# One-pass shift products in the last normalisation, and nine unread matrix products behind the output projection

## The chip, the cores and the metric

The kernel runs on one core of a Trainium2 chip. The metric is the device time in microseconds (us) of one execution, as the median over several runs. Profiles are of one execution each, and their times count from its first instruction.

## The reference

The program is one layer of an encoder with 512 tokens and 2048 features: an input projection, two kinds of attention with gates, an output projection, and at the end a residual and a layer normalisation. Only the end matters here:

```python
out = jnp.einsum('bse,ed->bsd', y, w_out[layer])
x = _layer_norm(DEEPNORM_ALPHA * x + out, ln_gain[layer], ln_bias[layer])

def _layer_norm(x, g, b):
    mu = xf.mean(-1, keepdims=True)
    var = jnp.square(xf - mu).mean(-1, keepdims=True)
    return (xf - mu) * lax.rsqrt(var + LN_EPS) * g + b
```

With the reciprocal deviation rs and z = ALPHA x + out, a row of the output is z·g·rs + (−mu·rs)·g + b. The second and third terms, a column per token times the gain row plus the bias row, are called the shift below. It has rank two.

## The kernel before

**Stages.** The core works through input projections (a Strassen scheme), attention with the gates and part of the output projection as filler, and then the output projection alone. There the tokens lie in four tiles of 128 (`t` 0 to 3) and the features in four groups of 512 (`dc` 0 to 3). Half of the contraction has been summed earlier into `z[t][dc]`; the rest runs over units `u` 4 to 7. The groups `dc` 0 and 1 are done for all tiles first. Then all weights of `dc` 2 and 3 are held in SBUF as `wts` (tiles `wlast`), and the loop goes tile by tile: 24 matmuls of 512 columns for `dc` 2, 24 for `dc` 3, then the tile's normalisation on VectorE while TensorE goes on with the next tile. The very last group, `t` 3 and `dc` 3, is done in two halves of 256 columns in two PSUM banks (48 matmuls).

**Number kinds.** A matmul operand of fp32 precision is split into a high and a low part of kind fp32r by `split` (ScalarE copies the high part, VectorE subtracts), and three fp32r matmuls stand for one of fp32. Only a few small products are plain fp32; among them are the transpose and the three shift products of the last tile.

**The last tile.** Nothing is left for TensorE to do beside tile 3's normalisation, so `last_norm` (L889) gives part of it to TensorE. Groups 0, 1 and 2 of the tile have been multiplied by the gain before the mean is known. Once `bn_aggr` (L894), the root on ScalarE (L895) and the reciprocal (L911) are there, VectorE writes −mu·rs into column 0 of `nms` (L912); column 1 holds ones since the start of the kernel. TensorE transposes `nms` (L914), ScalarE copies the result to `left` (L917), and three products of two rows each (L920) make the shift of groups 2, 0 and 1 from `rows`. Those rows are the gain and bias as they lie in memory, fetched by six DMAs of 2 KB in `shift_rows` (L886). VectorE meanwhile does group 3 without them (`centre`, L899, then `rescale`, L905), and then `rescale` of groups 2 and 0 and of group 1 in two halves, each reading its shift from PSUM. Each `rescale` issues one store of its result, on the queues of SyncE and ScalarE in turn (L908).

**Order.** In the loop over the last tiles VectorE's order is the written one (`manual_schedule` for that engine); the orders of TensorE, ScalarE, GpSimd and of SyncE's DMA queue are laid down at build time by the framework's scheduler from a simulated timeline. `shift_rows` stands in the program after the fetches of x and before the eight fetches of `wts` (L954), outside the manual part.

**Space.** `slot("h0")` to `slot("h5")` are the buffers in which split weights rotate up to group 1; the shift rows and `left` reuse `h1`, `h2` and `h3`, so they wait for the last matmuls that read those. `u0` held temporaries of the attention. PSUM has banks `acc` (4), `sc` (2, pool `pss`) and `pt` (2, pool `pst`).

Of the kernel before, what the change touches and what calls it, by code (L numbers as in the profile page):

```python
# [6 lines left out]
F32 = mybir.dt.float32  # L7
F32R = mybir.dt.float32r
BF16 = mybir.dt.bfloat16
AF = mybir.ActivationFunctionType  # L10
ALU = mybir.AluOpType
# [48 lines left out]
def _view(t, offset, dims):  # L60
    return bass.AP(tensor=t.tensor, offset=t.offset + offset, ap=dims)
# [2 lines left out]
BLOCKS = (("k", 0), ("q", 0), ("v", 0), ("k", 1), ("q", 1), ("v", 1))  # L64
ORDER = [(m % 2, m // 2) for m in range(2 * PAIRS)]
EARLY = 6
BIAS = ((0, 24), (192, 32), (448, 24))
BW = 640


def hybrid_layer(tc, xT, xn, w_in, w_early, w_gate, w_out, t5x, brow, rpb, cmask, eye, gain, lbias, out):
    nc = tc.nc
    from contextlib import ExitStack
    with ExitStack() as ctx:
        const = ctx.enter_context(tc.tile_pool(name="const", bufs=1))
        arena = ctx.enter_context(tc.tile_pool(name="arena", bufs=1))
        small = ctx.enter_context(tc.tile_pool(name="small", bufs=4))
        dram = ctx.enter_context(tc.tile_pool(name="dram", bufs=1, space=bass.MemoryType.DRAM))
        pacc = ctx.enter_context(tc.tile_pool(name="pacc", bufs=4, space=bass.MemoryType.PSUM))
        pss = ctx.enter_context(tc.tile_pool(name="pss", bufs=2, space=bass.MemoryType.PSUM))  # L80
        pst = ctx.enter_context(tc.tile_pool(name="pst", bufs=2, space=bass.MemoryType.PSUM))

        def f(ap):
            return ap.bitcast(F32)

        def split(raw, hi, lo):
            nc.scalar.activation(hi, raw, AF.Copy)
            nc.vector.tensor_tensor(lo, raw, f(hi), ALU.subtract)
# [5 lines left out]
        def slot(tag, dtype=F32, name=None):  # L94
            return arena.tile([128, sizes[tag[0]]], dtype, name=name or tag, tag=tag)
# [10 lines left out]
        def bank(pool, name):  # L106
            tag = {id(pacc): "acc", id(pss): "sc", id(pst): "pt"}[id(pool)]
            return pool.tile([128, 512], F32, name=name, tag=tag)
# [13 lines left out]
        idle = bank(pss, "sc")  # L122
# [3 lines left out]
        ident = const.tile([128, 128], F32, name="ident")  # L126
# [37 lines left out]
        def prep_b(g):  # L164
# [13 lines left out]
            def table(v):  # L178
                r, masks = held
                w, o = BIAS[v][1], 16 if v == 0 else 8  # L180
                gt = slot("b1", F32, "gt")[:, :15 * w].rearrange("p (d j) -> p d j", d=15)
# [4 lines left out]
            def write(v):  # L186
                at, w = BIAS[v]
                for k in range(8):
# [14 lines left out]
        for tag, n, ops in (("s0", 4, A5), ("s1", 4, A5), ("c0", 2, A6), ("c1", 2, A6),  # L203
                            *((f"n{i}", 1, A6) for i in range(4)), *((f"n{i}", 1, A3) for i in range(4, 12))):
            t = slot(tag, F32R, "op").rearrange("p (n s q) -> p n s q", n=n, s=2)
# [61 lines left out]
        def plain_block(src):  # L267
# [3 lines left out]
            accs = [bank(p, "acc") for p in (pacc, pacc, pacc, pacc, pss, pss)]  # L271
            width = 128 * EARLY

# [9 lines left out]
            for i in range(8):  # L283
                xr = slot(f"r{i}", F32, "xraw")[:, :1024].rearrange("p (s q) -> p s q", s=2)
                raws.append(xr)
                for s in range(2):
                    k, n = i + 8 * s, 2 * i + s
                    if n == 0:
# [16 lines left out]
                        split(raw[:, far], w[0][:, far], w[1][:, far])  # L305
                        for jj in (range(2), range(2, EARLY)):
                            for c in (slice(0, HALF), slice(HALF, S)) if jj[0] == 0 else (slice(0, S),):
# [6 lines left out]
                    if n < 14:  # L314
                        for j in range(EARLY):
                            mms(n, k, w, j)
# [169 lines left out]
        sg_out, sg_ring, rc_ring, y_ring = Ring("n6"), Ring("n8", "n9"), Ring("n10", "n11"), Ring("n5", "n7")  # L486
        stream = [w_gate[i] for i in range(2 * (2 * PAIRS - EARLY))] + [w_out[8 * dc + u] for dc in range(4) for u in range(4)]
        raw_ring, raws, ready = Ring("r8", "r9", "c0", "c1"), [], []
# [125 lines left out]
        def scores(n):  # L614
# [14 lines left out]
            if g == 0:  # L629
                p, exponent = softmax(sc, biases[h][:, 48 - 16 * b:560 - 16 * b], 512, 0, i, 4 * a + b)  # L630
                probs[n] = p, 4
                return exponent
            at = BIAS[(0, 1, 1, 2)[b]][0]
            outer = {0: (64, outers[h % 2][0]), 3: (0, outers[h % 2][1])}
# [70 lines left out]
        yk, z = [], []  # L705
# [5 lines left out]
        def out_mms(acc, t, u, wh, wl, first, last, part=slice(0, 512)):  # L711
            c = slice(t * 128, t * 128 + 128)
            for kk in range(2):
                k = 2 * u + kk
                wk = slice(kk * 512 + part.start, kk * 512 + part.stop)
                for n, (s, w) in enumerate(((0, wh), (1, wh), (0, wl))):
                    nc.tensor.matmul(acc[:, part], yk[k][:, s, c], w[:, wk], start=first and kk == 0 and n == 0,  # L717
                                     stop=last and kk == 1 and n == 2)
                    yield
# [20 lines left out]
        def fillers():  # L740
            for j in range(EARLY, 2 * PAIRS):
                yield from gate_unit(j)
            z.extend([] for _ in range(4))
            for dc in range(4):
                yield from out_first(dc)
# [21 lines left out]
        with tc.manual_schedule(engines=engines):  # L767
# [6 lines left out]
            for n in range(136):  # L774
                b, i = n % 4, n // 8
# [14 lines left out]
                if mixing:  # L790
                    if exponent:
                        exponent()
                    mine, theirs, y, t = values(n // 4 - 1)
# [28 lines left out]
        for tiles, src, first in ((gb, gain, 0), (bb, lbias, 6)):  # L822
            for i in range(4):
                t = slot(f"n{first + i}", F32, "gain")
# [54 lines left out]

        def shift_rows():  # L880

            groups = slot("h1", F32, "lnrows"), slot("h2", F32, "lnrows")
            groups = groups[0][:, :512], groups[0][:, 512:], groups[1][:, :512]
            for r, src in enumerate((gain, lbias)):
                for c in range(3):
                    nc.sync.dma_start(groups[c][r:r + 1], src[:, 512 * c:512 * c + 512])  # L886
            return groups

        def last_norm(rows):  # L889

            t = 3
            mv = small.tile([128, 2], F32, name="mv", tag="mv")
            rs = small.tile([128, 1], F32, name="rs", tag="rs")
            nc.vector.bn_aggr(mv, st[t])  # L894
            nc.scalar.activation(rs, mv[:, 1:2], AF.Sqrt, bias=eps)  # L895

            def centre(i):
                zt = z[t][i]
                nc.vector.scalar_tensor_tensor(zt, zt, mv[:, 0:1], gb[i], op0=ALU.subtract, op1=ALU.mult)  # L899

            queues = [nc.sync, nc.scalar]

            def rescale(i, part, by):
                zt = z[t][i][:, part]
                nc.vector.scalar_tensor_tensor(zt, zt, rs, by, op0=ALU.mult, op1=ALU.add)  # L905
                queue = queues.pop(0)
                queues.append(queue)
                queue.dma_start(out[384:512, 512 * i + part.start:512 * i + part.stop], zt)  # L908

            whole = slice(0, 512)  # L910
            nc.vector.reciprocal(rs, rs)  # L911
            nc.vector.scalar_tensor_tensor(nms[:, 0:1], mv[:, 0:1], -1.0, rs, op0=ALU.mult, op1=ALU.mult)  # L912
            flat = bank(pst, "pt")[0:2, 0:128]
            nc.tensor.transpose(flat, nms, ident)  # L914
            shifts = []
            left = slot("h3", F32, "lnleft")[0:2, 0:128]
            nc.scalar.activation(left, flat, AF.Copy)  # L917
            for i in (2, 0, 1):
                c = bank(pacc, "acc")
                nc.tensor.matmul(c, left, rows[i][0:2], start=True, stop=True)  # L920
                shifts.append(c)
            centre(3)
            rescale(3, whole, bb[3])
            rescale(2, whole, shifts[0])
            rescale(0, whole, shifts[1])
            for part in (slice(0, 256), slice(256, 512)):
                rescale(1, part, shifts[2][:, part])
# [17 lines left out]
        load_x(1)  # L945

        rows = shift_rows()
        nms = small.tile([128, 2], F32, name="nms", bufs=1)
        nc.gpsimd.memset(nms, 1.0)
        wts = {}  # L950
        for dc in (2, 3):
            for u in range(4, 8):
                raw = out_ring.next("wraw")
                nc.sync.dma_start(raw[:, :1024], w_out[8 * dc + u])  # L954
                i = 2 * (u - 4)
                wts[dc, u] = [slot(f"{'tr'[dc - 2]}{i + m}", F32R, "wlast") for m in range(2)]
                split(raw[:, :1024], *wts[dc, u])
        for t in range(4):
            for dc in (2, 3):
                acc = bank(pacc, "acc") if dc == 2 else bank((pss, pst)[t % 2], "acc")  # L960
                parts = (slice(0, 256), slice(256, 512)) if (t, dc) == (3, 3) else (slice(0, 512),)
                accs = [acc] if len(parts) == 1 else [acc, bank(pss, "sc")]
                for o, part in zip(accs, parts):
                    for u in range(4, 8):
                        list(out_mms(o, t, u, *wts[dc, u], u == 4, u == 7, part))
                with tc.manual_schedule(engines={mybir.EngineType.DVE}):
                    if (t, dc) == (0, 2):
                        for i in range(2):
                            nc.vector.tensor_tensor(z[3][i], z[3][i], gb[i], ALU.mult)
                    residual(dc, t)  # L970
                    for m, part in enumerate(parts):
                        finish(dc, t, accs[m], part, dc + m)
                    if (t, dc) == (3, 2):
                        nc.vector.tensor_tensor(z[t][2], z[t][2], gb[2], ALU.mult)
                    if dc == 3 and t < 3:
                        norm(t)
                    elif dc == 3:
                        last_norm(rows)


def _weights(w_in, w_out):
# [11 lines left out]
    gate = [4096 * g + 3072 + 128 * j for g, j in ORDER]  # L993
    early = np.concatenate([w[order][:, :, c:c + 128] for c in gate[:EARLY]], axis=2)
    blocks = []
# [42 lines left out]
```

## Time and profile before

| | |
|---|---|
| median of 3 runs | 978.78 us (977.58 to 978.81) |
| the profiled execution's own time | 979.85 us |
| its span, first to last instruction | 978.1 us |
| granted TensorE clock, mean | 0.996 |
| TensorE busy | 968.9 us, 99% |
| VectorE busy | 753.8 us, 77% |
| ScalarE busy | 484.5 us, 50% |

The span is 1.75 us shorter than the execution's own time, because that also holds what lies around the first and last instruction. PE is TensorE, PEld its weight loads, DVE VectorE, ACT ScalarE, POOL GpSimd, SPq and ACTq the sequencers of SyncE and ScalarE as they issue DMAs. A busy share says little about a stage: for each stage one reads which wait ends last.

### The profile page before, as it was taken

To read this page: it belongs to the slowest core of one execution; us is meant where nothing else is said; L and a number is where in the kernel's file an instruction comes from. 1 tells how busy PE (TensorE), PEld (TensorE's weight loads), DVE (VectorE), ACT (ScalarE), POOL (GpSimd) and SP (SyncE) were. 2 spreads that over 40 slices of the span, in tenths; PEclk is the share of its full clock that TensorE was granted. 3 is DMA by queue.
4 is the path that set the end of the run, shared out by engine and by line. 5 is a ranking of instruction groups with operands and counts; after the bars stand their busy time and mean duration, and the time that the engine had idled before them with its cause. 6 is when DMAs were issued, how large, how long until landed. Compare 5 with 4: busy or idle time off the path is not lost.

```text
span 978.1 us, 13605 instructions
## 1 busy us (share of the span) xinstructions
PE 968.9 (99%) x4639; PEld 799.2 (82%) x4639; DVE 753.8 (77%) x1150; ACT 484.5 (50%) x837; POOL 180.2 (18%) x325
## 2 busy tenths in 40 slices
PE   9999999999999999999999999999999999999996
PEld 7887888888888888888888888888888888888885
DVE  7948788787988968978889567676776867778876
ACT  7544344334445434434454366666766666764200
POOL 1000665663553600000000001010011001000020
PEclk9999999999999999999999999999999999999998
DMA  9831788679769628527634967777768688769222
GB/s 345 297 108 60 173 253 264 205 232 253 204 191 301 183 86 270 144 93 214 157 125 125 348 180 213 207 228 228 193 206 247 186 235 217 192 224 312 66 78 95
DMA packets 116034, 194.13 MB, mean 198 GB/s; under 512 B 46373, under 2 KB 65573, under 8 KB 115964
## 3 DMA queue, kind: packets, MB, share of 16 engines
q1 hardware_dynamic: 103132, 169.13, 56.6%
q0 software_dynamic: 12256, 23.47, 8.8%
q8 instruction: 37, 0.61, 0.3%
q10 hardware_dynamic: 576, 0.66, 0.2%
q14 instruction: 33, 0.27, 0.1%
HBM read 148.69 MB, written 44.50 MB: 198 GB/s over the span
## 4 chain that ended last, share of the span: by engine, by line
PE 97%; ACT 1%; DVE 1%; issue 0%; POOL 0%; DVEq 0%; ACTq 0%; POOLq 0%
PE acc L389 16%; PE acc L391 16%; PE acc L390 16%; PE acc L717 14%; PE acc L523 11%; PE pv L669 4%; PE pt L647 4%; PE acc L278 2%; PE acc L279 2%; PE acc L280 2%; PE sc L628 2%; PE sc L627 2%; PE pt L259 1%; PE sc L717 1%; PE pt L717 1%; PE acc L920 0%
## 5 line engine op out<-in xcount | busy, mean ns | idle before, releaser
L372 ACT ACTIVATE wh<-braw 128x1024 fp32r<-128x1024 f32 x168 | 178.4, 1062 | 254.7 <-PE acc L390 203.6
L377 DVE TENSOR_TENSOR wl<-braw,wh 128x1024 fp32r<-128x1024 f32 x168 | 206.2, 1230 | 53.7 <-ACT wh L372 52.1
L389 PE MATMUL acc<-wh,xk 128*128 128x512 f32 x384 | 151.9, 396 | 0.0
L391 PE MATMUL acc<-wl,xk 128*128 128x512 f32 x384 | 149.8, 390 | 0.0
L390 PE MATMUL acc<-wh,xk 128*128 128x512 f32 x384 | 149.6, 390 | 0.0
L368 DVE TENSOR_TENSOR braw<-braw 128x1024 f32<-128x1024 f32 x96 | 116.8, 1217 | 0.0
L389 PE MATMUL acc<-wh,op 128*128 128x512 f32 x288 | 112.8, 392 | 0.0
L391 PE MATMUL acc<-wl,op 128*128 128x512 f32 x288 | 112.2, 390 | 0.0
L390 PE MATMUL acc<-wh,op 128*128 128x512 f32 x288 | 112.1, 389 | 0.0
L717 PE MATMUL acc<-wh,yk 128*128 128x512 f32 x320 | 108.2, 402 | 0.0
L653 DVE TENSOR_TENSOR tl<-pt,th 128x256 fp32r<-128x256 f32 (+1 forms) x128 | 71.0, 555 | 48.1 <-ACT th L652 46.7
L652 ACT ACTIVATE th<-pt 128x256 fp32r<-128x256 f32 (+1 forms) x128 | 62.4, 490 | 64.9 <-PE pt L647 62.8
L523 PE MATMUL acc<-xk,wh 128*128 128x512 f32 x320 | 90.8, 402 | 0.0
L391 PEld LDWEIGHTS acc<-wl,xk 128*128 128x128 f32 x384 | 72.1, 188 | 15.4
L389 PEld LDWEIGHTS acc<-wh,xk 128*128 128x128 f32 x384 | 72.1, 188 | 15.1 <-ACT bias L150 0.9
L390 PEld LDWEIGHTS acc<-wh,xk 128*128 128x128 f32 x384 | 72.2, 188 | 14.3
L584 DVE CUSTOM_DVE_ANT_0 s<-sc,biases 128x512 f32<-128x512 f32 (+2 forms) x128 | 68.0, 531 | 17.9 <-PE sc L628 17.3
L588 ACT ACTIVATE p<-s,mn 128x512 f32<-128x512 f32 (+1 forms) x96 | 62.1, 647 | 25.5 <-DVE mn L584 25.2
L717 PEld LDWEIGHTS acc<-wh,yk 128*128 128x128 f32 x320 | 58.4, 189 | 8.9
L523 PEld LDWEIGHTS acc<-xk,wh 128*128 128x128 f32 x320 | 57.0, 189 | 9.5
L160 POOL DMA_DIRECT2D bias<-rows_d x128 | 61.5, 487 | 17.3 <-DMA bias<-rows_d 5.5
L717 PE MATMUL acc<-wl,yk 128*128 128x512 f32 x160 | 64.0, 403 | 0.0
(164 smaller groups left out, 1656.1 us busy)
## 6 DMA issues: line engine op xcount, KB each, us to landing
braw<-in_w_in SPq DMA_DIRECT2D x96, 512.0 KB
wraw<-in_w_out SPq DMA_DIRECT2D x32, 512.0 KB
wraw<-in_w_gate SPq DMA_DIRECT2D x20, 512.0 KB
k_d<-kst SPq DMA_DIRECT2D x64, 128.0 KB
q_d<-kst SPq DMA_DIRECT2D x64, 128.0 KB
v_d<-vst SPq DMA_DIRECT2D x32, 256.0 KB
q<-q_d SPq DMA_DIRECT2D x32, 256.0 KB
k<-k_d SPq DMA_DIRECT2D x16, 512.0 KB
```

What stands on the lines that cost most here:

```text
L368: nc.vector.tensor_tensor(raws[q][u], raws[q][u], raws[other][u], ALU.add)
L372: nc.scalar.activation(h, raws[q][u], AF.Copy)
L377: nc.vector.tensor_tensor(l, raws[q][u], f(h), ALU.subtract)
L389: nc.tensor.matmul(accs[t], ah[:, q], h[:, c], start=k == 0, stop=False)
L390: nc.tensor.matmul(accs[t], al[:, q], h[:, c], start=False, stop=False)
L391: nc.tensor.matmul(accs[t], ah[:, q], l[:, c], start=False, stop=k == 7)
L523: nc.tensor.matmul(acc, w[:, k * 128:k * 128 + 128], X[8 * u + k][:, s], start=u == 0 and n == 0 and k == 0, stop=u == 1 and n == 2 and k ...
L584: nc.vector.tensor_tensor_reduce(*flat, bias, 1.0, 3e38, ALU.add, ALU.min, mn)
L588: nc.scalar.activation(p[:, to:to + n].rearrange("p (b r c) -> p b r c", r=8, c=c), s[:, :n].rearrange(order, r=8, c=c), AF.Exp, bias=mn, ...
L652: nc.scalar.activation(th, pt[:, :nch], AF.Copy)
L653: nc.vector.tensor_tensor(tl, pt[:, :nch], f(th), ALU.subtract)
L717: nc.tensor.matmul(acc[:, part], yk[k][:, s, c], w[:, wk], start=first and kk == 0 and n == 0, stop=last and kk == 1 and n == 2)
```

## The change

`shift_rows` fetches gain and bias in another layout: column 4c to 4c+3 of `raw` (gain) and 12 further (bias) hold four features of group c on each of the 128 partitions. `raw` is split into high and low parts of kind fp32r, and fifteen DMAs from SBUF to SBUF lay these out again as five rows for each of the three groups: gain high, gain low, gain high, bias high, bias low. In `last_norm` −mu·rs is written to a small tile `nm`, rounded to fp32r into columns 0 and 1 of `nms`, and the remainder goes into column 2; the other columns hold ones. The transpose yields eight rows instead of two, and the three products are fp32r with five rows. Behind the last matmul of the output projection stand nine more fp32r matmuls of 512 columns, into a bank `sc` that nothing reads.

```diff
+AWAKE = 9
 ...
         def shift_rows():
-            groups = slot("h1", F32, "lnrows"), slot("h2", F32, "lnrows")
+            raw, parts = slot("u0", F32, "lnraw"), slot("h0", F32R, "lnparts")
+            for i, src in enumerate((gain, lbias)):
+                nc.sync.dma_start(raw[:, 12 * i:12 * i + 12].rearrange("p (c j) -> p c j", c=3),
+                                  _view(src, 0, [[4, 128], [512, 3], [1, 4]]))
+            split(raw[:, :24], parts[:, :24], parts[:, 24:48])
+            groups = slot("h1", F32R, "lnrows"), slot("h2", F32R, "lnrows")
             groups = groups[0][:, :512], groups[0][:, 512:], groups[1][:, :512]
-            for r, src in enumerate((gain, lbias)):
+            for r, at in enumerate((0, 24, 0, 12, 36)):
                 for c in range(3):
-                    nc.sync.dma_start(groups[c][r:r + 1], src[:, 512 * c:512 * c + 512])
+                    nc.sync.dma_start(f(groups[c][r:r + 1]), f(parts[:, at + 4 * c:at + 4 * c + 4]))
             return groups
 ...
+            nm = small.tile([128, 1], F32, name="nm", tag="nm")
 ...
-            nc.vector.scalar_tensor_tensor(nms[:, 0:1], mv[:, 0:1], -1.0, rs, op0=ALU.mult, op1=ALU.mult)
-            flat = bank(pst, "pt")[0:2, 0:128]
-            nc.tensor.transpose(flat, nms, ident)
+            nc.vector.scalar_tensor_tensor(nm, mv[:, 0:1], -1.0, rs, op0=ALU.mult, op1=ALU.mult)
+            nc.vector.tensor_copy(nms[:, 0:2], nm.to_broadcast([128, 2]))
+            nc.vector.tensor_tensor(nms[:, 2:3], nm, f(nms[:, 0:1]), ALU.subtract)
+            flat = bank(pst, "pt")[0:8, 0:128]
+            nc.tensor.transpose(flat, f(nms), ident)
 ...
-            left = slot("h3", F32, "lnleft")[0:2, 0:128]
+            left = slot("h3", F32R, "lnleft")[0:8, 0:128]
 ...
-                nc.tensor.matmul(c, left, rows[i][0:2], start=True, stop=True)
+                nc.tensor.matmul(c, left[0:5], rows[i][0:5], start=True, stop=True)
 ...
-        nms = small.tile([128, 2], F32, name="nms", bufs=1)
-        nc.gpsimd.memset(nms, 1.0)
+        nms = small.tile([128, 8], F32R, name="nms", bufs=1)
+        nc.gpsimd.memset(f(nms), 1.0)
 ...
+                if (t, dc) == (3, 3):
+                    idle = bank(pss, "sc")
+                    for _ in range(AWAKE):
+                        nc.tensor.matmul(idle, yk[8][:, 0, 0:128], wts[3, 4][0][:, 0:512], start=True, stop=True)
```

## The prediction

> **What bounds the kernel now.** First the page's chain that ended last, then the chain piece by piece from 940 us on, then engines and granted clock by stage.
>
> ```profile
> PE 97%; ACT 1%; DVE 1%; issue 0%; POOL 0%; DVEq 0%; ACTq 0%; POOLq 0%
> ...
> 922.07 23.12 PE acc L717 x102
> ...
> 963.02 2.89 PE sc L717 x24
> 965.91 0.02 issue
> ...
> 966.85 0.30 DVE mv L894
> ...
> 967.18 0.30 ACT rs L895
> ...
> 967.51 0.17 DVE rs L911
> 967.68 0.02 issue
> 967.70 0.17 DVE nms L912
> 967.87 0.04 issue
> 967.92 0.28 PE pt L914
> ...
> 968.23 0.28 ACT lnleft L917
> ...
> 968.54 4.21 PE acc L920 x6
> ```
>
> Columns are start, length and what. Until 965.91 PE alone sets the time: 102 matmuls in 23.12 us, one each 0.227 us, no gap. What the change can win lies in the 12.2 us behind. There the chain is one of short steps, and one long piece, the shift products, 4.21 us. How much of that VectorE feels is in its own rows (start, duration, what, idle time before).
>
> ```profile
> 967.78 0.74 DVE L899 SCALAR_TENSOR_TENSOR z<-z,mv,gain 128x512 f32<-128x512 f32 x1
> 968.56 0.75 DVE L905 SCALAR_TENSOR_TENSOR z<-z,rs,gain 128x512 f32<-128x512 f32 x1
> 969.70 0.75 DVE L905 SCALAR_TENSOR_TENSOR z<-z,rs,acc 128x512 f32<-128x512 f32 x1 [0.39 <-PE acc L920]
> 971.07 0.75 DVE L905 SCALAR_TENSOR_TENSOR z<-z,rs,acc 128x512 f32<-128x512 f32 x1 [0.62 <-PE acc L920]
> 972.78 0.87 DVE L905 SCALAR_TENSOR_TENSOR z<-z,rs,acc 128x256 f32<-128x256 f32 x2 [0.96 <-PE acc L920]
> 973.18 0.47 DVE L905 SCALAR_TENSOR_TENSOR z<-z,rs,acc 128x256 f32<-128x256 f32 x1
> ```
>
> VectorE waits three times for a product, 0.39 + 0.62 + 0.96 = 1.97 us, and ends at 973.65. That is all that faster products can bring it, not 4.21 us. Behind it come the stores; here are their issues and, by quarter microseconds, the load of PE, PEld, DVE, ACT and POOL, then granted clock, DMA share and GB/s.
>
> ```profile
> 969.34 4.67 SPq L908 DMA_DIRECT2D out<-z  x3
> 970.49 3.15 ACTq L908 DMA_DIRECT2D out<-z  x2
> 973.68 0.33 SPq L908 DMA_DIRECT2D out<-z  x1
> ...
> 969.50:969.75 0.25, 0.25 (x2) 0.18 (x1) 0.05 (x1) 0.00 (x0) 0.00 (x0) 1.00 0.00 0
> 969.75:970.00 0.25, 0.25 (x2) 0.02 (x1) 0.25 (x1) 0.00 (x0) 0.00 (x0) 0.77 0.00 0
> 970.00:970.25 0.25, 0.25 (x2) 0.25 (x1) 0.25 (x1) 0.00 (x0) 0.00 (x0) 0.50 0.23 90
> 970.25:970.50 0.25, 0.25 (x1) 0.06 (x1) 0.20 (x1) 0.00 (x0) 0.00 (x0) 0.50 1.04 393
> 970.75:971.00 0.25, 0.25 (x2) 0.17 (x1) 0.00 (x0) 0.00 (x0) 0.00 (x0) 0.50 0.48 172
> 971.00:971.25 0.25, 0.25 (x2) 0.17 (x1) 0.18 (x1) 0.00 (x0) 0.00 (x0) 0.50 0.00 0
> 974.75:975.00 0.25, 0.00 (x0) 0.00 (x0) 0.00 (x0) 0.00 (x0) 0.00 (x0) 0.50 0.71 242
> 975.00:975.25 0.25, 0.00 (x0) 0.00 (x0) 0.00 (x0) 0.00 (x0) 0.00 (x0) 0.50 0.00 0
> ```
>
> A store's data flow some 0.87 us behind its issue (969.34, to about 970.2) at up to 393 GB/s, so 256 KB take 0.67 us, and between two stores the DMA engines now stand still. The last data flow until about 974.93, 1.28 us behind VectorE's end; the remaining 3.2 us to 978.1 are landing and closing, which the change leaves alone. The clock is full until 969.75 and half from 970.0.
>
> **The change, part by part.**
>
> *Two more small steps ahead of the transpose.* The row of `nm` takes the place of L912; a copy of two columns and a subtraction of one follow, each needing the one before. From L911 to L912, likewise dependent, it is 967.70 − 967.51 = 0.19 us from start to start. Neither step is in the trace; the bounds are 0.08 each, the gap from L912 to the independent L899 behind it, and 0.33, from L894 to L895 across engines. They stay on one engine and depend on each other, so I take 0.19 each. `nms` is ready at 967.87 + 0.38 = 968.25, and `centre` of group 3 starts at 967.78 + 0.38 = 968.16. This is a loss of 0.38 us on VectorE's path, hidden by nothing.
>
> *Transpose and copy.* Eight rows instead of two change neither the 128 streamed columns nor the copied ones: 0.28 and 0.28 as before, with the same gaps, so the first product starts at 968.54 + 0.38 = 968.92.
>
> *The products.* Six records stand for three products, two each; an fp32r product is one record.
>
> ```profile
> L717 PE MATMUL acc<-wlast,yk 128*128 128x512 f32 x168 | 38.2, 389 | 0.0
> L920 PE MATMUL acc<-lnrows,lnleft 2*128 2x512 f32 x6 | 4.2, 854 | 0.4 <-ACT lnleft L917 0.4
> 969.08 0.18 PEld L920 LDWEIGHTS acc<-lnrows,lnleft 2*128 2x128 f32 x1 [0.24 <-issue]
> ```
>
> With five rows it isn't in the trace. Its bounds are 0.39 us, the mean of 128 rows, and 1.16 us, the wait from 968.54 to VectorE's start at 969.70. I take 0.18 for the weights plus 0.39, as the rows say of the same kind with more rows: the shifts are ready at 969.49, then 0.227 us apart, 969.72 and 969.94.
>
> *VectorE then.* Dependent operations start 0.78 apart (967.78 to 968.56); for independent ones the row is one from the normalisation of the tile before.
>
> ```profile
> 960.79 0.74 DVE L856 SCALAR_TENSOR_TENSOR z<-z,rs,gain 128x512 f32<-128x512 f32 x1
> 961.45 0.74 DVE L852 SCALAR_TENSOR_TENSOR z<-z,mv,gain 128x512 f32<-128x512 f32 x1
> ```
>
> 0.66 to 0.67. So `centre` 968.16, `rescale` of group 3 968.94, group 2 969.61, group 0 970.28, group 1 970.95 and 971.35, end 971.82. Each shift is there 0.12, 0.56 and 1.01 us before it is read: the waits of 1.97 us go. Of the three product waits 0.38 us is given back by the small steps, and some 0.24 us is recovered by operations that now overlap at their ends: 973.65 − 971.82 = 1.83 us earlier.
>
> *The stores are late next.* They are issued at 969.72, 970.40, 971.06, 971.46 and 971.85. Data of the first flow from 970.59; at 0.67 us for each of three, and 0.33 for each half, the engines run without a pause until 970.59 + 2.67 = 973.26, which the last store alone, 971.85 + 0.87 + 0.33 = 973.05, would not need. So 0.2 us of the gain stays in the queue: 974.93 − 973.26 = **1.67 us**. Halves have rows of 1 KB; in the trace both took 0.75 us (974.18 to 974.93) rather than 0.67, which makes the gain 1.6. I take 1.6.
>
> *Nine unread matmuls.* At 0.227 us they take 2.04, from 965.91 to 967.95. `nms` comes at 968.25, so they lie in PE's wait, with 0.3 us to spare. Their bank was last read by tile 2, whose data VectorE took at 954.75. Cost nothing; if that cover fails, at most 2.04 us, if they stood ahead of the last matmuls. Their worth is near nothing too. Without them the clock would halve at about 969.88 again, when the three products have all started (968.92, 969.15, 969.37).
>
> Trainium skill, "TensorE: Matmul & The Clock Gate", part 1: after at least one idle window of about 3.4 us the clock falls to half, and the windows run free, so the moment can differ between runs. The trace shows the fall 3.97 us behind PE's last full work and does not show where the window began. By that rule the fall could come as early as 965.91 + 3.4 = 969.3 without the nine, and with them not before the products end; by the row nothing is won, and by the page at most one late product, 0.2 us, that VectorE reads only 1.01 us later. The sum is 1.6 us by both.
>
> *Fetching and splitting the rows.* Two fetches and fifteen copies between SBUF rows replace six fetches on SP's queue; one small ACT copy and one small DVE subtraction are new (0.27 and 0.16 by the nearest rows, L917 and L912), long before 968 and off PE's path. On SP stands behind them the last weight fetch, L954.
>
> ```profile
> 911.22 0.55 SPq L886 DMA_DIRECT2D lnrows<-in_gain  x2
> 914.89 0.35 SPq L954 DMA_DIRECT2D wraw<-in_w_out  x1
> 916.43 0.23 SPq L886 DMA_DIRECT2D lnrows<-in_gain  x1
> 919.08 1.23 DVE L88 TENSOR_TENSOR wlast<-wraw,wlast 128x1024 fp32r<-128x1024 f32 x1 [2.36 <-ACT wlast L87]
> 932.99 0.69 DVE L842 TENSOR_TENSOR z<-acc,z 128x512 f32<-128x512 f32 x1 [4.02 <-PE acc L717]
> L243 SPq DMA_DIRECT2D k_d<-kst x64: 574/605/1021, 130.2 to 407.1; - x64
> ```
>
> The weight is ready at 920.31 and first read by the last six matmuls of tile 0's group 3, at 932.97 − 6·0.227 = 931.6: 11.3 us of slack. The split can start when `h0` is free, as `h1` is, at 911.2, so copies start near 911.9. Issues of DMAs with several dimensions take 0.605 us here (extremes 0.574 and 1.021; a single row 0.23). Fifteen take 9.1 us: all of them ahead of L954 move it from 914.89 to 921, 6.1 late, and 5.2 us of slack are left. They cost nothing.
>
> *Sum.* 1.6 us. Against the profiled execution: span 976.5, own time 979.85 − 1.6 = 978.25. The median shown, 978.78, lies 1.07 us under that execution's own time; carried over, 978.78 − 1.6 = **977.2 us**. A measurement of this kernel tells about 0.2%, 1.96 us, from no change: 976.8 and 980.7.
>
> **The rivals.**
>
> *More than the sum (faster).* If the two small steps overlap like L912 and L899, at 0.08 us each, VectorE ends at 971.60; and if the stores' last data end 1.28 us behind it as now, the gain is 2.05 us: **976.7**. For it: every small operation in these rows overlaps where it may. Against: the steps depend on each other, and the stores have no pause left to save.
>
> *The products keep their length.* If five-row fp32r products took what fp32 takes at full clock, 1.16 us for the first and 0.91 for each further (4·0.227), the shifts come at 970.08, 970.99 and 971.90, VectorE ends at 972.77, the gain is 0.88: **977.9**. Against: 168 rows of 389 ns.
>
> *The nine stand in the way.* TensorE's order is laid down by the scheduler; if they came ahead of the last real matmuls, or the transpose waited for them, up to 2.04 us is lost again: 977.2 + 2.0 = **979.2**. Against: they stand last in the program and real matmuls never wait.
>
> *The row copies hold up the last weight (slower).* PE stalls in tile 0 once fifteen issues at x us end so late that the weight comes behind 931.6: 911.9 + 15x − 914.89 > 11.3, from x = 0.95. The gain is gone at 1.06, and at 1.2 the stall is 3.7 us: 977.2 + 3.7 = **980.9**. For it: the longest issue in L243 is 1.021 us, and other work in SP's order could be put behind the copies too. Against: the median is 0.605.
>
> **How the numbers follow.** The forecast, 976.9 to 977.7 by its own bounds: 0.50. More than the sum: 0.28. Products keep their length: 0.05. The nine in the way: 0.08. The weight held up: 0.09. Faster by over 0.2% is the second case, 0.28; slower the last, 0.09; the others are within, 0.63. The range reaches down past 976.7 to 976.3, as runs shown differ by 1.2 us, and up to the nine in the way, 979.2; the last case stays out.
>
> **What the next profile would show.** Three L920 records near 0.39 us instead of six; VectorE without a wait for PE behind `centre`, ending near 971.8; DMA share near 1.0 from 970.6 to 973.3 without a pause; nine matmuls on `sc` between 965.9 and 968, the transpose starting with `nms`; a full clock during the products; L954's last issue by 921 and no PE idle at 931. Wrong would be: a wait in L905, a pause of PE before 965.9, PE's last real matmul at another time than 965.9 from a shifted order, or an end of the span more than 3.5 us behind the last data.

## The result, and the profile after

The changed kernel takes 976.92 us (median of 22 runs, 976.32 to 978.22); the kernel before, run beside it, 978.79 (22 runs, 977.28 to 981.37). The ratio is 0.9982, 95% interval 0.9975 to 0.9988: faster by 1.87 us, against 1.6 forecast for a time of 977.2. More striking than the medians is the scatter: 4.1 us from fastest to slowest before, 1.9 after.

The new lines have other numbers: the last `centre` is L906, `rescale` L912, its stores L915, the three products L929, the nine unread ones L978, the copies of the rows L892, the weight fetches L963. First the tail of the changed kernel in order of time.

```profile
965.46 2.23 PE L978 MATMUL sc<-wlast,yk 128*128 128x512 f32 x9
965.66 0.42 DVE L843 TENSOR_TENSOR z<-sc,z 128x256 f32<-128x256 f32 x1 [1.22 <-PE sc L718]
...
967.24 0.16 DVE L918 RECIPROCAL rs<-rs 128x1 f32<-128x1 f32 x1 [0.36 <-ACT rs L902]
967.43 0.16 DVE L919 SCALAR_TENSOR_TENSOR nm<-mv,rs 128x1 f32<-128x1 f32 x1
967.63 0.17 DVE L920 CAST nms<-nm 128x2 fp32r<-128x2 f32 x1
967.83 0.16 DVE L921 TENSOR_TENSOR nms<-nm,nms 128x1 fp32r<-128x1 f32 x1
967.91 0.74 DVE L906 SCALAR_TENSOR_TENSOR z<-z,mv,gain 128x512 f32<-128x512 f32 x1
968.04 0.28 PE L923 MATMUL pt<-ident,nms 128*8 128x128 f32 x1 [0.35 <-DVE nms L921]
968.36 0.27 ACT L926 ACTIVATE lnleft<-pt 8x128 fp32r<-8x128 f32 x1 [1.15 <-PE pt L923]
968.68 0.97 PE L929 MATMUL acc<-lnrows,lnleft 5*128 5x512 f32 x3 [0.36 <-ACT lnleft L926]
968.69 0.75 DVE L912 SCALAR_TENSOR_TENSOR z<-z,rs,gain 128x512 f32<-128x512 f32 x1
969.36 2.18 DVE L912 SCALAR_TENSOR_TENSOR z<-z,rs,acc 128x512 f32<-128x512 f32 x4
969.47 2.43 SPq L915 DMA_DIRECT2D out<-z  x3
```

The three products are three records in 0.97 us, where there were six in 4.21. VectorE's four operations that read a shift run as one block with no wait and end at 969.36 + 2.18 = 971.54. TensorE's last real matmul ends 0.27 us sooner in this execution than in the one before (965.64 against 965.91; 0.12 us of that is there at 44 us already, in matmuls that the change doesn't touch), so times are best counted from there: VectorE ends 5.9 us behind it, where it was 7.74. The stores, by quarter microseconds (the last three columns are clock, DMA share and GB/s):

```profile
970.00:970.25 0.25, 0.00 (x0) 0.00 (x0) 0.25 (x2) 0.00 (x0) 0.00 (x0) 1.00 0.00 0
970.25:970.50 0.25, 0.00 (x0) 0.00 (x0) 0.25 (x1) 0.00 (x0) 0.00 (x0) 1.00 0.75 287
970.75:971.00 0.25, 0.00 (x0) 0.00 (x0) 0.25 (x2) 0.00 (x0) 0.00 (x0) 1.00 0.87 311
...
971.50:971.75 0.25, 0.00 (x0) 0.00 (x0) 0.04 (x1) 0.00 (x0) 0.00 (x0) 0.98 1.05 402
971.75:972.00 0.25, 0.00 (x0) 0.00 (x0) 0.00 (x0) 0.00 (x0) 0.00 (x0) 0.50 1.01 361
...
973.00:973.25 0.25, 0.00 (x0) 0.00 (x0) 0.00 (x0) 0.00 (x0) 0.00 (x0) 0.50 0.75 250
973.25:973.50 0.25, 0.00 (x0) 0.00 (x0) 0.00 (x0) 0.00 (x0) 0.00 (x0) 0.50 0.08 25
973.50:973.75 0.25, 0.00 (x0) 0.00 (x0) 0.00 (x0) 0.00 (x0) 0.00 (x0) 0.50 0.05 16
973.75:974.00 0.25, 0.00 (x0) 0.00 (x0) 0.00 (x0) 0.00 (x0) 0.00 (x0) 0.50 0.00 0
```

The pauses between stores are gone, the clock holds until 971.74, 2 us past the last product, and the bulk of the data is out at 973.3. A thin rest, 0.08 and 0.05 of the 16 engines, goes on to about 973.7; it matters below. The span ends at 975.1, 1.8 us behind the bulk, where the profile before has 3.2.

### The profile page after: what moved, and what is told of

It reads as the page before. It is cut to its first block, busy times and chain, and to the rows that moved or that the text cites. A ratio compares the mean times of both kernels' runs of the same rounds, so it can differ in the third digit from the quotient of the medians.

```text
span 975.1 us, 13637 instructions
## 1 busy us (share of the span) xinstructions
PE 967.3 (99%) x4645; PEld 799.8 (82%) x4645; DVE 753.4 (77%) x1153; ACT 484.8 (50%) x838; POOL 178.0 (18%) x325
## 4 chain that ended last, share of the span: by engine, by line
PE 96%; DVE 1%; ACT 1%; DMA 0%; issue 0%; DVEq 0%; ACTq 0%
PE acc L390 16%; PE acc L392 16%; PE acc L391 16%; PE acc L718 14%; PE acc L524 11%; PE pv L670 4%; PE pt L648 4%; PE acc L279 2%; PE acc L280 2%; PE acc L281 2%; PE sc L629 2%; PE sc L628 2%; PE pt L260 1%; PE sc L718 1%; PE pt L718 1%; DMA xraw<-in_xT 0%
```

## The experiments

Two runs on different chips differ by some tenths of a microsecond, so each group has its own yardstick. Differences below are between medians, with 95% intervals from resampling the runs.

**Group 1: the two halves of the change.** The change again, unaltered:

> The change itself once more, on the chip of the three runs below, as their yardstick. By my theory (waits of 1.97 us for products go, 0.4 us go to two more small steps, stores then queue) it is again 1.5 to 2.0 us faster than the kernel before, ratio 0.998. The rival, that part of the measured gain was luck in how long the last stores take to land (3.2 us from the last data to the end of the span in the profile before, 1.8 in the one after), would let this profile show another stretch there, up to 1.4 us longer, with the rest unchanged.

977.38 us (12 runs, 977.05 to 978.14) against 979.24 before (33 runs, 976.94 to 981.1): ratio 0.9980 (0.9972 to 0.9989). Again 1.86 us. From the last bulk data (973.9) to the end of the span (975.6) it is 1.7 us, much as in the first profile of the change, so the 3.2 us of the profile before don't belong to every execution.

The five rows without the nine:

```diff
-AWAKE = 9
+AWAKE = 0
```

> The five fp32r rows without the nine unread products. My theory: the nine are worth nothing beside the fp32r rows; the time is that of the change within 0.2 us, VectorE again without a wait for a product, while the clock falls to half about 3.9 us behind TensorE's last real matmul, that is near 969.6, as the products end. The rival, that the nine hold the clock and the products need it: some product comes late, VectorE waits 0.2 us or more and the time rises by as much.

977.15 us, 0.23 below the change (interval −0.71 to 0.46): the nine are worth nothing that shows in the median (group 4 has something that goes with them). Here the profile of it:

```profile
968.86 1.22 PE L929 MATMUL acc<-lnrows,lnleft 5*128 5x512 f32 x3 [0.36 <-ACT lnleft L926]
969.54 2.18 DVE L912 SCALAR_TENSOR_TENSOR z<-z,rs,acc 128x512 f32<-128x512 f32 x4
...
969.25:969.50 0.25, 0.25 (x3) 0.13 (x1) 0.25 (x1) 0.00 (x0) 0.00 (x0) 0.74 0.00 0
969.50:969.75 0.25, 0.25 (x2) 0.00 (x0) 0.25 (x2) 0.00 (x0) 0.00 (x0) 0.50 0.00 0
```

The clock falls at about 969.38, 3.56 us behind the last real matmul (965.82) and in the middle of the products. They take 1.22 instead of 0.97 us, and VectorE's block is 2.18 as before, without a wait: the late end of the products is not felt by anyone.

The nine with the old rows and products:

```diff
+                if (t, dc) == (3, 3):
+                    idle = bank(pss, "sc")
+                    for _ in range(AWAKE):
+                        nc.tensor.matmul(idle, yk[8][:, 0, 0:128], wts[3, 4][0][:, 0:512], start=True, stop=True)
```

> The nine unread products with the two-row fp32 products and the old rows. My theory: here the nine are worth something, since the fp32 products now run at full clock to the end: three products 0.91 us apart, ready 1.16, 2.07 and 2.98 us after the copy, VectorE ends about 1.3 us sooner than before (972.4 against 973.65) and the time falls by 1.2 us, ratio 0.9988. The rival, that the nine do nothing at all: the clock falls to half as before, ratio 1.000, VectorE still waits 1.97 us. A second rival: the nine hold back the transpose, ratio above 1.000.

977.9 us, ratio 0.9985 (0.9977 to 0.9994): 1.3 us faster than before, and 0.5 slower than the change (−0.01 to 0.89). So what the nine are worth depends on what stands behind them.

```profile
968.70 3.64 PE L921 MATMUL acc<-lnrows,lnleft 2*128 2x512 f32 x6 [0.36 <-ACT lnleft L918]
968.72 0.75 DVE L906 SCALAR_TENSOR_TENSOR z<-z,rs,gain 128x512 f32<-128x512 f32 x1
969.86 1.60 DVE L906 SCALAR_TENSOR_TENSOR z<-z,rs,acc 128x512 f32<-128x512 f32 x2 [0.40 <-PE acc L921]
972.38 0.87 DVE L906 SCALAR_TENSOR_TENSOR z<-z,rs,acc 128x256 f32<-128x256 f32 x2 [0.91 <-PE acc L921]
...
970.50:970.75 0.25, 0.25 (x2) 0.23 (x1) 0.14 (x2) 0.00 (x0) 0.00 (x0) 0.71 0.94 360
```

The clock fell at about 970.6, 1.9 us behind the start of the products, where it was 1.3 in the profile before: later, but not late enough for the third. VectorE's waits shrink from 1.97 to 1.3 us. I had expected full clock to the end; by its mean clock, 0.997, this execution is among the three of the 12 in which it fell soonest (the others have 0.998 and 0.999). In the 3.41 us ahead of the fall, 967.19 to 970.60, TensorE was busy for 3.05, most of it with the transpose and the products of two rows; that did not hold the clock.

That the 1.3 us are the clock's is not shown. Counted from TensorE's last real matmul, VectorE ends only 0.5 us sooner here than in the profile before (7.20 us behind it against 7.74), while the span ends 1.8 us sooner (10.36 against 12.17). The rest goes with an instruction fetch, which stands in the last stores of the profile before (see below) and at 969.8 us here, ahead of most of them. No run separates the two causes, and the twelve times don't follow the clock: they are 978.3, 977.4 and 978.0 us on average at 0.997, 0.998 and 0.999.

Eighteen instead of nine (`AWAKE = 18`):

> The change with eighteen unread products instead of nine. My theory: nine end 0.3 us ahead of the transpose, and eighteen, 2.04 us longer, no longer fit: the transpose starts 1.7 us later, VectorE waits 1.65 us for the first shift, the stores lose their queue, and the end comes 1.1 to 1.3 us later than that of the change. The rival, that unread products cost TensorE nothing because they are still somewhere in its slack: no later than the change.

978.57 us, 1.2 above the change (0.9 to 1.4), as expected; VectorE waits 1.28 us for its first shift, where I had 1.65.

```profile
967.73 0.16 DVE L921 TENSOR_TENSOR nms<-nm,nms 128x1 fp32r<-128x1 f32 x1
969.46 0.27 PE L923 MATMUL pt<-ident,nms 128*8 128x128 f32 x1
970.62 2.19 DVE L912 SCALAR_TENSOR_TENSOR z<-z,rs,acc 128x512 f32<-128x512 f32 x4 [1.28 <-PE acc L929]
```

`nms` is written by 967.89 and the transpose starts at 969.46: unread matmuls are free only as long as they end before the next real one could start.

**What the scatter of the kernel before is made of.** Each run also gives the mean granted clock of its span. A mean of 0.996 over 978 us is about 7.8 us at half clock, so a lower mean says that more time followed the fall. The table has the 92 runs of the kernel before that stand beside the experiments, and the 22 of the five rows without the nine, sorted by it; they are from several chips.

| mean clock | before: runs, mean us | five rows, no nine: runs, mean us |
|---|---|---|
| 0.994 | 4, 981.8 | |
| 0.995 | 35, 980.1 | |
| 0.996 | 23, 979.1 | 5, 977.2 |
| 0.997 | 21, 978.4 | 11, 977.2 |
| 0.998 | 9, 977.9 | 6, 977.1 |

In the kernel before the time goes with the clock, by up to 4 us. The spans do too: 980.0 us on average at 0.994 and 976.0 at 0.998, which puts the fall near 968 us in the first and near 972 in the last, an estimate from these means. With one-pass products the time doesn't follow, at clocks from 0.996 to 0.998. That is a correlation; the next two runs set the clock down in every execution.

**Group 2: the clock always down.** Seven unread VectorE operations ahead of the shift row, in the kernel before and in that with five rows and no nine:

```diff
             nc.vector.reciprocal(rs, rs)
+            for _ in range(7):
+                nc.vector.tensor_tensor(junk, gb[3], bb[3], ALU.add)
```

> The kernel before with seven unread VectorE operations of 512 columns (about 4.2 us) between the reciprocal and the shift row, so that TensorE's wait is longer than its clock lasts. Theory: the fp32 products cost what the clock makes of them. All three now run at half clock in each execution: besides 4.2 us the end moves by 1.0 to 1.3 us more (products 1.7 us apart, waits of VectorE 4.0 us and more instead of 1.97), about 984.5 us where the kernel before has 979.2, and the scatter of the kernel before (4.2 us from fastest to slowest) shrinks to about 1.5 us, because the moment of the fall no longer matters. Rival: the scatter of the kernel before has to do with something else (the stores' landing, the start of the kernel) and stays; the time rises by 4.2 us alone.

> The same seven operations in the kernel with five fp32r rows and no unread products. Theory: one-pass products at half clock still end ahead of VectorE but for the first, which comes 0.1 to 0.3 us late; so 4.2 to 4.5 us above the same kernel without the seven (977.2 on the chip of the runs above), about 981.5, and 2.8 to 3.2 us below the fp32 one with the seven. Rival: the fp32r products suffer from half clock as the fp32 ones do, and the distance between the two is the 1.8 us of the change, or less.

985.29 us (984.59 to 986.16) and 982.1 us (981.67 to 982.91), beside 979.08 for the kernel before. The tails, of the fp32 kernel first and then of the fp32r one:

```profile
972.51 0.15 DVE L916 SCALAR_TENSOR_TENSOR nms<-mv,rs 128x1 f32<-128x1 f32 x1
973.45 5.49 PE L924 MATMUL acc<-lnrows,lnleft 2*128 2x512 f32 x6 [0.36 <-ACT lnleft L921]
975.55 0.75 DVE L907 SCALAR_TENSOR_TENSOR z<-z,rs,acc 128x512 f32<-128x512 f32 x1 [1.45 <-PE acc L924]
977.26 0.75 DVE L907 SCALAR_TENSOR_TENSOR z<-z,rs,acc 128x512 f32<-128x512 f32 x1 [0.96 <-PE acc L924]
978.97 0.87 DVE L907 SCALAR_TENSOR_TENSOR z<-z,rs,acc 128x256 f32<-128x256 f32 x2 [0.96 <-PE acc L924]
```

```profile
972.26 0.15 DVE L923 SCALAR_TENSOR_TENSOR nm<-mv,rs 128x1 f32<-128x1 f32 x1
973.59 1.65 PE L933 MATMUL acc<-lnrows,lnleft 5*128 5x512 f32 x3 [0.36 <-ACT lnleft L930]
974.42 2.19 DVE L914 SCALAR_TENSOR_TENSOR z<-z,rs,acc 128x512 f32<-128x512 f32 x4 [0.17 <-PE acc L933]
```

The seven took 4.8 us, not 4.2. At half clock the fp32 products take 5.49 us, 1.71 from one to the next, and VectorE waits 3.4 us; the fp32r ones take 1.65 and cost it 0.17. The time rose by 6.2 us in the one, 1.4 beyond the delay, and by 4.95 in the other (from 977.15, which is another chip's). The distance between the two is 3.2 us where the change is worth 1.9. On VectorE's path alone, from TensorE's last real matmul to VectorE's end, they differ by 2.98 us (13.97 and 10.99), and the profiles before and after by 1.84 (7.74 and 5.90). In size this is the theory's outcome, though I had put VectorE's waits at 4.0. The scatter is not: it is 1.6 us over the 5 runs of the fp32 kernel, but the kernel before has only 2.4 over 10 on this chip, and the standard deviations are 0.71 and 0.75. That a clock which is always down takes the scatter away isn't shown.

**Group 3: what is left on the path.** The yardstick on a third chip:

> The change, as yardstick on the same chip for the three runs below: ratio 0.998 to the kernel before.

976.97 us (976.62 to 977.24) against 979.4, ratio 0.9972 (0.9962 to 0.9983). The forecast of 0.998 lies at the edge of that interval; the kernel before had no clock above 0.997 here.

One VectorE step where the change has three; the low part of −mu·rs and its row are left out:

```diff
-            nc.vector.scalar_tensor_tensor(nm, mv[:, 0:1], -1.0, rs, op0=ALU.mult, op1=ALU.mult)
-            nc.vector.tensor_copy(nms[:, 0:2], nm.to_broadcast([128, 2]))
-            nc.vector.tensor_tensor(nms[:, 2:3], nm, f(nms[:, 0:1]), ALU.subtract)
+            nc.vector.scalar_tensor_tensor(nms[:, 0:2], mv[:, 0:1].to_broadcast([128, 2]), -1.0,
+                                           rs.to_broadcast([128, 2]), op0=ALU.mult, op1=ALU.mult)
```

> The change with one VectorE step instead of three for the transposed columns: the product of mean and reciprocal is written in fp32r into two columns at once, and its low part, with the third row of the rows (gain high once more), is left out. Theory: the two steps stand on the path and cost 0.40 us in the profile; everything behind them, stores included, moves by that: 0.3 to 0.45 us faster than the change. Rival: the stores' queue is the end, so VectorE's gain is lost there, and nothing changes.

977.02 us, 0.05 above the yardstick (−0.35 to 0.23): nothing came of it, though VectorE did what was expected; from TensorE's end to VectorE's end it is 5.5 us instead of 5.9. The profiled execution shows a place where it can have gone. By window, and the DMA queues at 969.7 to 970.7:

```profile
972.50:972.75 0.25, 0.00 (x0) 0.00 (x0) 0.00 (x0) 0.00 (x0) 0.00 (x0) 0.50 0.70 234
972.75:973.25 0.50, 0.00 (x0) 0.00 (x0) 0.00 (x0) 0.00 (x0) 0.00 (x0) 0.50 0.06 23
973.25:973.75 0.50, 0.00 (x0) 0.00 (x0) 0.00 (x0) 0.00 (x0) 0.00 (x0) 0.50 0.05 18
973.75:974.25 0.50, 0.00 (x0) 0.00 (x0) 0.00 (x0) 0.00 (x0) 0.00 (x0) 0.50 0.00 0
...
q8 instruction: 1, 0.02, 6.0%
```

The bulk of the data is out at 972.7, but a share of 0.06, which is one engine of 16, writes on until 973.65. At 969.71 one transfer of instructions starts, 16 KB in a single packet: 6.0% of 16 engines' microsecond, 0.96 us of one engine. That engine begins its part of the stores a microsecond after the others and ends it as much later. The profile after shows the same in a milder form, since its stores begin nearer to the fetch's end: fetch at 969.67, data from 970.3, the thin rest to 973.7. With the fetch where it was, sooner stores moved fifteen engines and not the sixteenth, in this one execution.

Group 3 of the last tile in two halves:

```diff
-            centre(3)
-            rescale(3, whole, bb[3])
+            for part in (slice(0, 256), slice(256, 512)):
+                centre(3, part)
+                rescale(3, part, bb[3][:, part])
```

> The change with group 3 of the last tile centred, rescaled and stored in two halves, so that the first store is issued about 0.6 us sooner; VectorE has two instructions more (about 0.3 us). Theory: behind VectorE the stores are a full queue of 2.95 us, so what counts is when the first can go and that the last is not late: 0.2 to 0.5 us faster than the change although VectorE ends later. Rival: VectorE's end counts, and the time rises by up to 0.3 us.

977.28 us, 0.31 above the yardstick (−0.06 to 0.61): no gain, and rather a loss, as the rival had it. The first store is issued 3.3 us behind TensorE's end instead of 3.8, but the second half comes only 0.92 us later, and a pause opens in the stores (DMA share 0.00 and 0.10 from 970.75 to 971.25):

```profile
968.90 0.48 DVE L912 SCALAR_TENSOR_TENSOR z<-z,rs,gain 128x256 f32<-128x256 f32 x1
969.82 0.48 DVE L912 SCALAR_TENSOR_TENSOR z<-z,rs,gain 128x256 f32<-128x256 f32 x1
970.22 2.19 DVE L912 SCALAR_TENSOR_TENSOR z<-z,rs,acc 128x512 f32<-128x512 f32 x4
```

VectorE makes 256 KB in 0.66 us and the engines write it in about 0.74 (2.95 us for four times as much); neither is clearly the bound, and an earlier start with the same rate behind it won nothing here.

All of it together, without the nine:

> One step (the low part of the shift left out) and the first store in halves, without the nine unread products. Theory: the two gains add, 0.4 to 0.9 us faster than the change, ratio to the kernel before 0.9972 to 0.9976; the missing nine cost nothing. Rival: with the wait shortened and the first group in halves, VectorE's end binds, and the sum is no better than the better of the two.

977.05 us, 0.08 above the yardstick (−0.05 to 0.67). The theory that the gains add has fallen with its two parts. The profiled execution is the slowest of the eleven, 979.69 us, and 2.95 us of that lie around its span. In it an instruction fetch starts at 978.98, 2.2 us behind the span's end at 976.74.

**Group 4: the fetch.** Does the saved step come through where no fetch falls into the stores?

> The five rows without the nine unread products once more, as yardstick for the next run. In the profile of this kernel no instruction fetch fell into the last stores; I expect none again, and a ratio of 0.9975 to 0.998 to the kernel before.

> One VectorE step for the transposed columns (the low part of the shift and its third row left out) without the nine. With the nine the 0.4 us that this saves on VectorE didn't reach the end: the profile has a 16 KB instruction fetch on one of the 16 DMA engines, ending at 970.7, and that engine then wrote its share of the last stores 0.9 us behind the others. Theory: where no fetch falls into the last stores, as in the kernel of the run above, the 0.4 us come through: 0.3 to 0.45 us faster than it, and its last packets end all within 0.2 us. Rival: the 0.4 us are lost whether or not a fetch is there, since landing and closing don't follow VectorE; then the two are equal within 0.15 us.

977.16 us (976.82 to 977.83) and 976.88 us (976.37 to 978.78), a difference of −0.27 (−0.57 to 0.56). In the two profiles no fetch falls behind 948 us, the last data of both end within 0.1 us, and the span is 0.3 us shorter with one step (975.1 and 974.8; the medians of all runs, 975.2 and 974.85, differ by 0.35, 0.05 to 0.60). But 4 of the 12 runs of the second kernel have 2.8 to 3.1 us around their span instead of 1.8, and 3 of the first 2.4 to 2.6. So: inside the span it went as the theory says, in the whole time it is not settled. No version clearly beats the change.

The time around the span goes with the place of the last such fetch, in all 14 profiles. Where it lies within the span, 1.77 to 1.87 us are around it (nine profiles); where no fetch comes behind 950 us, 1.94 to 2.05 (four); in the one where it comes behind the end, 2.95. It goes with the unread products as well: they put the last fetch at 965 to 970 us in all seven profiles that have them, and none of their 84 runs has more than 1.92 us around its span, while 30 of the 148 runs without them have over 2.2. So the nine do nothing for the median, but late runs of this kind are absent with them. That the fetch is the cause is not tested.

## Why the prediction was right, step by step

**The path of VectorE** came out as added up. From TensorE's last real matmul to VectorE's end I had 971.82 − 965.91 = 5.91 us; it is 971.54 − 965.64 = 5.90. The two small steps cost 0.20 each (I took 0.19), the first product starts 3.04 us behind TensorE's end (3.01), and no shift is waited for.

**The stores' queue** was the right next thing, a little too short: the data start 4.7 us behind TensorE's end as forecast, but take 2.95 us, not 2.67. They flow at some 355 GB/s with a full queue, where I had used the 393 of the single peaks. Cost: 0.3 us.

**"The remaining 3.2 us … which the change leaves alone"** is the term that failed, and it is larger than that 0.3. Counted from the bulk of the data the tail is 1.8 us in the profile after. In the profile before an instruction fetch stood in the last two stores:

```profile
q8 instruction: 1, 0.02, 6.0%
...
975.50:976.00 0.50, 0.00 (x0) 0.00 (x0) 0.00 (x0) 0.00 (x0) 0.00 (x0) 0.50 0.06 10
976.00:976.50 0.50, 0.00 (x0) 0.00 (x0) 0.00 (x0) 0.00 (x0) 0.00 (x0) 0.50 0.05 18
976.50:977.00 0.50, 0.00 (x0) 0.00 (x0) 0.00 (x0) 0.00 (x0) 0.00 (x0) 0.50 0.00 0
```

The first line is of the queues from 974.4 to 975.4. One engine was 1.4 us late, to 976.4. I read 974.93 as the last data because the rest was one sixteenth of the share. Counted from the very last packet (976.42 and 973.71) the tails are 1.66 and 1.41 us, and 1.4 to 1.8 in all 14 profiles: landing and closing do stay, and what went is the thin rest ahead of them. Between the two profiled executions the time fell by 2.94 us, 1.3 more than my sum. The execution before was 1.07 us above the median, which I carried over without asking for its cause, and that kept the error out of the forecast. That is luck. The fetch is not that execution's alone: the fp32 kernel with the seven operations has one in its last stores too (at 980.64 us, one engine 1.4 us late). With the nine in both kernels, where it comes by 970 us in each profile, the new products are worth 0.5 us (−0.01 to 0.89). The other 1.3 us of the median gain are what the nine are worth to the old products, and how much of these is VectorE's at a fallen clock and how much the fetch's, no run separates.

**The nine at no cost and no worth** held: they end at 967.69, `nms` comes at 967.99, 0.3 us to spare as worked out, and eighteen cost 1.2. What I had not seen is that they alone would have been worth 1.3 us to the old products, by the clock or by the fetch.

**The clock.** I took its fall at 969.88 as the kernel's, but it is that execution's. The Trainium skill, "TensorE: Matmul & The Clock Gate", part 1, says that the idle windows run free and that the transition varies between runs. The trace agrees: full clock began 4.2 to 9.9 us into the span, and then lasted 962.56, 965.97 or 969.38 us in each of the 14 profiles, lengths that are 3.41 us apart. So the moment of the fall depends on that of the rise. I applied this to the changed kernel, where it changes nothing, and not to the kernel before, where it moves three fp32 products. In the seven profiles without unread products the clock fell 2.2 to 5.1 us behind the last real matmul. The earliest fall that I took from the idle window of the Trainium skill, 3.4 us behind it, was no bound: in the fp32 kernel with the seven operations it came 2.20 us behind it (968.07 and 965.87), and in the 3.41 us ahead of the fall TensorE had been busy for 1.21. That the execution profiled lies near the middle of the table, with 0.996, helped my sum to come near the median gain; that too is luck.

**The rivals.** Products of the old length: three records of 392 to 499 ns say no. The nine in the way: they stand behind all real matmuls. The row copies holding up the last weight: fifteen issues of 0.595 us each (0.605 forecast), the last fetch at 921.9 (921 forecast), and the weight is split at 927.7. TensorE doesn't stall; the scheduler gave it other matmuls first, and group 3 of tile 0 ends 2 us later (934.98 against 932.99) without cost:

```profile
910.98 10.88 SPq L892 DMA_DIRECT2D lnrows<-lnparts  x15
921.91 0.58 SPq L963 DMA_DIRECT2D wraw<-in_w_out  x1
926.49 1.22 DVE L89 TENSOR_TENSOR wlast<-wraw,wlast 128x1024 fp32r<-128x1024 f32 x1 [1.16 <-ACT wlast L88]
```

More than the sum, at 976.7 us, came close: 1.87 us gained, just under the 0.2%. Its mechanism, small steps overlapping, is not what happened.

## What to carry to other kernels

A few plain fp32 matmuls behind a pause of TensorE can cost scatter, not only time: with one-pass products in their place the time no longer went with the moment at which the clock falls, and then holding the clock was worth nothing in the median. Before one adds unread work to hold a clock, one should ask whether the work behind it is still on the path at half clock. Unread work also moves the instruction fetches, so what it gains need not be the clock's. And a profile is one execution: where a kernel scatters by more than the change is worth, sort the runs by their granted clock, and look at the last thin share of the DMA engines before calling a tail fixed.

## What the runs showed of the hardware

One instruction fetch of 16 KB takes 0.92 to 1.22 us of one of the 16 DMA engines, in the ten profiles that have one behind 960 us, and if it falls into the last stores that engine ends up to 1.4 us behind the rest and sets the end. Its moment differs between executions of one kernel: in three profiles of the change it stands near 966, 969.7 and 969.6 us. These fetches come once per 253 recorded TensorE instructions on average (181 to 329) in the profile before, where the counts of VectorE between two of them range from 29 to 70 and those of ScalarE from 5 to 58; so they are probably TensorE's own. Its recorded instructions are 9412 in the kernel before, 9407 with the five rows alone and 9425 with the nine, and the last fetch came at 974.4 us, in none of two profiles, and at 966 to 970. That the count decides is not tested.

Of the runs without unread products, 16 of 92 of the kernel before and 14 of 56 of the others have 2.2 us and more around the span instead of 1.8, up to 3.25. The lengths of full clock differ by steps of 3.41 us. At half clock three shift products of two rows in fp32 take 5.49 us and three of five rows in fp32r 1.65; the latter take 0.97 at full clock.
